# Expert-choice MoE: an expert's list two experts ahead, its rows gathered one ahead and turned inside the preceding down product

## Chip, cores and metric

The kernel runs on one core of one Trainium2 chip. The metric is the device time of one execution in microseconds (us), the median of the runs.

## The reference, cut to what matters

One encoder layer: a norm, one projection, a mixture of dilated attention and a gated recurrence, an output projection, and then a mixture of experts in which each expert picks its own tokens. The change lies in this last part alone. S is 2048 tokens, D is 1024, there are 16 experts of hidden width 1024, and each takes cap = 256 tokens.

```python
def expert_choice_moe(h, w_router, w_gate, w_up, w_down):
    cap = max(1, CAPACITY_FACTOR * S // N_EXPERTS)
    logits = jnp.einsum('bsd,de->bse', h, w_router)
    aff = jax.nn.softmax(logits, axis=-1)
    gate, idx = lax.top_k(aff.transpose(0, 2, 1), cap)
    xin = jax.vmap(lambda hb, ib: hb[ib])(h, idx)
    hid = silu(einsum('becd,edf->becf', xin, w_gate)) * einsum('becd,edf->becf', xin, w_up)
    y = jnp.einsum('becf,efd->becd', hid, w_down) * gate[..., None]
    return jnp.zeros_like(h).at[bidx, idx].add(y)
```

## The kernel before, in words

Some 1680 us go by before the experts: norm and projection, recurrence, attention, output projection, router, and a search that finds for every expert the value that its 256th token has. Nothing in that part is touched. It leaves `post`, which holds for every token and expert the place in the expert's list (or none), `vals`, which holds token numbers and router weights in bf16 pieces, and `h2_d`, the normed tokens in DRAM.

Each expert then goes through these steps, which the names below refer to.

- **List** (`lists`, lines 1014 to 1035). For each of 16 groups of tokens VectorE compares `post` with a ramp and so makes a one-hot matrix `oh` (L1022), and TensorE multiplies two halves of it with `vals` (L1024, 32 small products into a bank of `mpt`). VectorE copies the sums out (`lv`, L1029) and forms the token numbers `ix` (L1032) and the weights `gate` (L1033, L1034).
- **Gather** (`gather`, L1041). Two indirect DMAs, issued from GpSimd (POOL), fetch 128 rows of 4 KB each from `h2_d` into the tiles `xg`.
- **Turning** (`xt_of`, lines 1046 to 1057). TensorE transposes the 2 x 8 blocks of `xg` into `mpt`, four to a bank (L1053); ScalarE writes the high part `xh` (L1055), VectorE the rest `xl` (L1056). Products are made of high and low parts, three for each pair of operands.
- **Gate product** (L1096 to L1098). Eight blocks `fb` of 128 hidden columns, each 2 x 24 products of 256 columns into one bank of `mpg` (two banks). After each block ScalarE takes the silu and VectorE the product `sg` (L1100, L1101), and the two write its parts `hh` and `hl` (L1102, L1103).
- **Down product** (L1129 to L1131). Eight blocks of 12 products of 512 columns, into the four banks of `mpy`. Then `add_rows` scales the result by `gate` (L1108, L1109) and adds it to the output by an indirect DMA from POOL (L1110).
- **Weights** (`w_split`). SP loads 1 MB at a time into `mraw` (three buffers), ScalarE writes the high part `mhi` (L1083), VectorE the low part `mlo` (L1084); six buffers each, two for every block of the gate product, one for every block of the down product.

The order on each engine is made by a scheduler: it simulates the program with its own cost model and lets the ready instruction that stands earliest in the code go first, as far as buffers are free. On the chip each engine then runs its own fixed order, and waits where an operand is late. In the code, list, gather and turning of expert e + 1 all stand ahead of expert e's products:

```python
nxt = ready(0)
for e in range(16):
    cur = nxt
    if e + 1 < 16:
        nxt = ready(e + 1)
    expert(e, *cur)
```

`ready` is list, gather and turning in a row, so all three are spread over the gate product of expert e, and the turning sits there at the place that the simulated gather allowed. The one-hots have three buffers, `xg` has three, `ix` and `gate` three.

Of the kernel before, what the change touches and what calls it, by code (L numbers as in the profile page):

```python
# [45 lines left out]
def encoder_layer(ctx, tc, x, norm1_w, w_in, q_norm_w, k_norm_w, lb_f, lb_b, o_norm_w, w_out,  # L46
# [4 lines left out]
    class Lane:  # L51
        """A range of scheduling priorities (lower goes first) for one stream of instructions."""
# [48 lines left out]
    # ones with a zero at the start of each chunk of 128  # L101
# [6 lines left out]
    def rsqrt(y, a, tmp):  # L108
        """y = a ** -0.5 to fp32 accuracy; a, y, tmp of one shape."""
        act.activation(y, a, AF.Ln)  # L110
        act.activation(y, y, AF.Exp, scale=-0.5)
        dve.tensor_mul(tmp, y, y)
        dve.scalar_tensor_tensor(tmp, tmp, -0.5, a, op0=OP.mult, op1=OP.mult)
        dve.scalar_tensor_tensor(y, tmp, 1.5, y, op0=OP.add, op1=OP.mult)

# [9 lines left out]
    def phase0(g):  # L125
        """tokens 256 g to 256 g + 255, scaled and turned; the low parts as lo_d has them"""
# [31 lines left out]
    # W columns  # L158
    AQ, AK, AV, HQ, HF, HB, HI, HG = [512 * i for i in range(8)]

    def prep(cols, kc):
        """hi and lo parts of two 128-column blocks of W_in with the norm's weight, k block kc"""
# [9 lines left out]
    def evac_qk(u):  # L172
        """columns of two heads' queries and keys: each head's normalised"""
# [30 lines left out]
    def project(cols, kind, ev, begin=False):  # L204
        """one unit of 256 columns; kind "t": tokens on partitions, "f": columns on partitions"""
# [59 lines left out]
    LEVELS = (64, 32, 16, 8, 4, 2, 1)  # L265

    def hg_setup(p):
# [20 lines left out]
        # lower bounds: row 0 of a softmax over two rows, per (direction, head)  # L288
# [25 lines left out]
    def hg_head(p, T, h):  # L314
# [7 lines left out]
        def gates(g, d):  # L322
            """ln f and softplus(z) of direction d; the latter gives the log of the key, ln(1 - lb) - softplus(z)"""
# [25 lines left out]
        # backward direction: E is the sum over the chunk's earlier positions; states after each chunk  # L349
# [22 lines left out]
        for g in range(4):  # L372
# [34 lines left out]
            def level(m):  # L407
                """key and query factors of both directions for pairs in opposite halves of 2m positions; m = 0:
                pairs of a position with itself"""
# [91 lines left out]
    def att_setup(p):  # L501
# [22 lines left out]
        # a column of ones after the values gives the denominators  # L524
# [5 lines left out]
    def att_load(p, T, h, g):  # L530
        """queries and keys of head h: tokens 512 g to 512 g + 511"""
        u, s2 = h // 2, h % 2
        for j in range(2):
            # each row twice, for both halves of the partitions
# [7 lines left out]
    def att_values(T, h, g):  # L542
        # keys of pattern 0 and 1 in blocks of 128, shifted by 64
# [13 lines left out]
    def att_turn(T, g):  # L557
        """columns on partitions: the query's high and low parts, the key's each twice"""
# [18 lines left out]
    def att_head(p, T, h):  # L577
# [8 lines left out]
        def unit(pat, n):  # L586
            """queries' first and stride, keys' first, first and last column, key blocks"""
# [56 lines left out]
        def four(pat, n4, nst):  # L644
            """four units of 128 queries: numerators, denominators and negated maxima"""
# [6 lines left out]
        # partition p of pattern 2 has tokens 16 p + r, of pattern 1 512 g + 4 p + r, of pattern 0 128 n + p;  # L652
        # they are put together in the order of pattern 1
        for g in range(4):
# [5 lines left out]
            # the next head's columns take their places as this head leaves them  # L660
# [41 lines left out]
    def op_setup(op):  # L702
# [8 lines left out]
        # the lower and the upper 16 bits of the gates, as numbers  # L711
# [12 lines left out]
    def op_mm(T, c, half, src, bank):  # L724
        """adds the contribution of mixed's column half to src's tokens"""
# [32 lines left out]
    def op_tile(T, c):  # L758
# [21 lines left out]
        # the norm's scale of a token comes after the product  # L780
# [110 lines left out]
    # the digits' candidates; the third enters negated and half a step lower  # L891
# [39 lines left out]
    def search(v, digits):  # L931
        """the largest whole number that at least CAP of an expert's numbers reach, in base 4"""
        cand, cur = kk[:, digits - 1, :], None
        for i in range(digits - 1, -1, -1):
# [5 lines left out]
            # twice the count less 256, a whole number of at most 256  # L940
# [26 lines left out]
    # the upper bits; then the lower ones among those whose upper bits are the ones found, above or below them the rest  # L967
# [7 lines left out]
    # places: the strictly greater, then those equal as long as there are places  # L975
# [38 lines left out]
    def lists(e):  # L1014
        """token indices and gates of expert e's slots"""
        pl = pt2()
        n = 0
        for hf in range(2):
            for sg in range(8):
                col = e * 8 + sg  # L1020
                oh = mp.tile([128, CAP], BF, name="oh", bufs=3)
                dve.tensor_scalar(oh, iotb, post[:, hf * 128 + col:hf * 128 + col + 1], None, op0=OP.is_equal)  # L1022
                for sh in range(2):
                    pe.matmul(pl[:, sh * 8:sh * 8 + 5], oh[:, sh * 128:(sh + 1) * 128], vals[:, hf, col, :],  # L1024
                              start=n == 0 and sh == 0, stop=n == 15, skip_group_check=True)
                n += 1
# [3 lines left out]
        ix = mp.tile([128, 2], I32, name="ix", bufs=3)  # L1030
        gt_ = mp.tile([128, 2], F32, name="gate", bufs=3)
# [3 lines left out]
        return ix, gt_  # L1035

    def gather(ix):
        xg = []
        for s in range(2):
            t = mp.tile([128, D], F32, name="xg", bufs=3)  # L1040
            pool.indirect_dma_start(out=t, out_offset=None, in_=h2_d,  # L1041
                                    in_offset=bass.IndirectOffsetOnAxis(ap=ix[:, s:s + 1], axis=0))
            xg.append(t)
        return xg

    def xt_of(xg):
        xh = mp.tile([128, KC, 256], F32R, name="xh", bufs=2)
        xl = mp.tile([128, KC, 256], F32R, name="xl", bufs=2)
        for kq in range(4):
            p = pt2()  # L1050
            for j in range(4):
                k, s = kq * 2 + j // 2, j % 2
                pe.transpose(p[:, j * 128:(j + 1) * 128], xg[s][:, k * 128:(k + 1) * 128], ident)  # L1053
            pv_ = p.rearrange("p (k t) -> p k t", k=2)
            act.activation(xh[:, kq * 2:kq * 2 + 2, :], pv_, AF.Copy)  # L1055
            dve.tensor_sub(xl[:, kq * 2:kq * 2 + 2, :], pv_, xh[:, kq * 2:kq * 2 + 2, :].bitcast(F32))  # L1056
        return xh, xl
# [3 lines left out]
    def w_raw(e, kind, i):  # L1061
        """raw weights: gate / up, two 128-column blocks; down, two 128-row blocks"""
# [24 lines left out]
    def expert(e, xh, xl, ix, gate):  # L1087
        hh = mp.tile([128, KC, 256], F32R, name="hh", bufs=1)
        hl = mp.tile([128, KC, 256], F32R, name="hl", bufs=1)
        for fb in range(KC):  # L1090
# [12 lines left out]
            dve.tensor_sub(hl[:, fb, :], sg, hh[:, fb, :].bitcast(F32))  # L1103
        py = [mps.tile([128, 512], F32, name="mpy", bufs=4) for _ in range(4)]
# [8 lines left out]
        # the last expert's second half comes later, so that the first half's rows are added meanwhile  # L1113
        lag = 3 if e == 15 else 0
        wd = {}
        for fb in range(KC + lag):
# [3 lines left out]
            for s in range(2):  # L1120
# [5 lines left out]
                for n in range(2):  # L1126
# [4 lines left out]
                    pe.matmul(o, hl[:, f, ts], hi[:, cs], start=False, stop=f == KC - 1)  # L1131
            if fb == KC - 1:
                add_rows(0)
        add_rows(1)

    def ready(e):
# [36 lines left out]
```

## Time and profile before

| | us |
|---|---|
| runs | 2863.09, 2871.4, 2881.84 |
| median | 2871.4 |
| profiled execution, first to last instruction | 2869.1 |
| TensorE busy in it | 2746.1 (96%) |
| experts: first gate product to last down product | 1680.6 to 2855 |

No time of its own is given for the profiled execution beside its span; the span lies between the lowest and the highest of the three runs, 2.3 us below their median. A busy TensorE in the profile need not be one at its peak: a product that starts while the one before it still runs counts once, and what shows the rate is the distance from one start to the next.

### The profile page before, as it was taken

Reading aid. Unit: us, or ns where it says so; the run is one execution under the profiler, and the core shown is the slowest. Engines: PE = TensorE matmul, PEld = TensorE weight load, DVE = VectorE, ACT = ScalarE, POOL = GpSimd, SP = SyncE. Lnnn points to the kernel's source line nnn. Section 1 sums busy time; section 2 is a strip of 40 time slices with the busy share of each in tenths; the row PEclk is TensorE's granted clock in tenths of the full one; section 3 lists DMA queues with packets and bytes.
Section 4 is the critical chain, followed back from the end, with each engine's and each line's share of the span. In section 5 each row is a group of like instructions: output and inputs, shape, how many; then the busy total and the mean of one; then the engine's idle time right before and its main releaser. Section 6 shows DMA issues by size and latency. Waiting matters only on the chain. (4 is left out here: it accounts for less than half of the span.)

```text
span 2869.1 us, 59634 instructions
## 1 busy us (share of the span) xinstructions
PE 2746.1 (96%) x23462; PEld 2585.8 (90%) x23462; DVE 1780.8 (62%) x4396; ACT 1456.3 (51%) x2829; POOL 131.2 (5%) x157
## 2 busy tenths in 40 slices
PE   8999999999999999999999769999999999999998
PEld 8999998999999999988998669999989999999997
DVE  6637887888865446755666665555555555555553
ACT  6636666676655444634455434444444444444442
POOL 0000000000000000000000000000000000000000
PEclk9999999999999999989999879999999999999999
DMA  9877767777686554645548436666666666666663
GB/s 301 259 243 215 235 209 222 215 222 231 206 236 186 148 141 132 173 136 164 155 110 291 139 113 193 198 203 205 206 205 186 197 198 199 205 204 201 200 202 105
DMA packets 557064, 558.75 MB, mean 195 GB/s; under 512 B 142944, under 2 KB 507488, under 8 KB 556784
## 3 DMA queue, kind: packets, MB, share of 16 engines
q1 hardware_dynamic: 547248, 521.31, 58.2%
q0 software_dynamic: 9536, 33.64, 5.4%
q8 instruction: 184, 3.01, 0.4%
q14 instruction: 96, 0.79, 0.1%
HBM read 453.92 MB, written 100.93 MB: 193 GB/s over the span
## 5 line engine op out<-in xcount | busy, mean ns | idle before, releaser
L1084 DVE TENSOR_TENSOR mlo<-mraw,mhi 128x1024 fp32r<-128x1024 f32 x384 | 470.2, 1225 | 399.9 <-ACT mhi L1083 399.5
L1083 ACT ACTIVATE mhi<-mraw 128x1024 fp32r<-128x1024 f32 x384 | 406.8, 1060 | 517.7 <-PE mpg L1097 328.0
L1096 PE MATMUL mpg<-xh,mhi 128*128 128x256 f32 x2048 | 584.6, 286 | 0.0
L1097 PE MATMUL mpg<-xl,mhi 128*128 128x256 f32 x2048 | 582.6, 285 | 0.0
L1098 PE MATMUL mpg<-xh,mlo 128*128 128x256 f32 x2048 | 579.8, 283 | 0.0
L1096 PEld LDWEIGHTS mpg<-xh,mhi 128*128 128x128 f32 x2048 | 387.5, 189 | 0.5 <-ACT xh L1055 0.4
L1097 PEld LDWEIGHTS mpg<-xl,mhi 128*128 128x128 f32 x2048 | 386.8, 189 | 0.0
L1098 PEld LDWEIGHTS mpg<-xh,mlo 128*128 128x128 f32 x2048 | 386.5, 189 | 0.0
L236 PE MATMUL pm<-whi,hth 128*128 128x256 f32 x1280 | 367.9, 288 | 12.8 <-ACT est L200 9.7
L237 PE MATMUL pm<-wlo,hth 128*128 128x256 f32 x1280 | 366.3, 286 | 3.6 <-DVE wlo L169 3.3
L238 PE MATMUL pm<-whi,hlo 128*128 128x256 f32 x1280 | 366.7, 287 | 0.0
L236 PEld LDWEIGHTS pm<-whi,hth 128*128 128x128 f32 x1280 | 245.3, 192 | 15.8 <-ACT est L200 12.0
L237 PEld LDWEIGHTS pm<-wlo,hth 128*128 128x128 f32 x1280 | 245.2, 192 | 5.8 <-DVE wlo L169 5.0
L238 PEld LDWEIGHTS pm<-whi,hlo 128*128 128x128 f32 x1280 | 245.0, 191 | 0.4
L238 PE MATMUL pm<-hth,wlo 128*128 128x256 f32 x768 | 220.6, 288 | 4.2 <-DVE wlo L169 4.2
L236 PE MATMUL pm<-hth,whi 128*128 128x256 f32 x768 | 220.8, 288 | 2.4 <-ACT est L200 2.3
L237 PE MATMUL pm<-hlo,whi 128*128 128x256 f32 x768 | 219.3, 286 | 0.0
L1131 PE MATMUL mpy<-mhi,hl 128*128 128x512 f32 x512 | 202.9, 396 | 0.0
L1130 PE MATMUL mpy<-mlo,hh 128*128 128x512 f32 x512 | 202.9, 396 | 0.0
L1129 PE MATMUL mpy<-mhi,hh 128*128 128x512 f32 x512 | 202.3, 396 | 0.0
L641 PEld LDWEIGHTS pn<-vp,eT 128*128 128x128 f32 (+1 forms) x1280 | 168.0, 194 | 15.9 <-DVE eT L622 2.6
L641 PE MATMUL pn<-vp,eT 128*128 128x65 f32 (+1 forms) x1280 | 179.8, 278 | 2.5 <-DVE eT L622 2.1
(328 smaller groups left out, 5436.8 us busy)
## 6 DMA issues: line engine op xcount, KB each, us to landing
hlo<-lo_d SPq DMA_DIRECT2D x480, 256.0 KB, 4.1
mraw<-in_w_expert_gate_dram SPq DMA_DIRECT2D x64, 1024.0 KB, 5.2
mraw<-in_w_expert_up_dram SPq DMA_DIRECT2D x64, 1024.0 KB, 5.3
mraw<-in_w_expert_down_dram SPq DMA_DIRECT2D x64, 1024.0 KB, 5.2
wraw<-in_w_in_dram SPq DMA_DIRECT2D x128, 128.0 KB, 4.2
out_dram<-oxt SPq DMA_DIRECT2D x32, 512.0 KB, 4.0
pf_d<-est SPq DMA_DIRECT2D x96, 128.0 KB, 3.8
cb<-num_d SPq DMA_DIRECT2D x32, 264.0 KB, 3.1
```

The costliest lines, as they stand in the source:

```text
L236: pe.matmul(o, l[0], r[0], start=kc == 0, stop=False)
L237: pe.matmul(o, l[0], r[1], start=False, stop=False)
L238: pe.matmul(o, l[1], r[0], start=False, stop=kc == KC - 1)
L641: pe.matmul(pnum[:, n0 % 4 + j, :], eT[:nk, c:c + 128], vp[:nk, b, :], start=i == 0, stop=i == nb - 1)
L1083: act.activation(hi, src, AF.Copy)
L1084: dve.tensor_sub(lo, src, hi.bitcast(F32))
L1096: pe.matmul(o, hi[:, k, :], xh[:, k, :], start=k == 0, stop=False)
L1097: pe.matmul(o, hi[:, k, :], xl[:, k, :], start=False, stop=False)
L1098: pe.matmul(o, lo[:, k, :], xh[:, k, :], start=False, stop=k == KC - 1)
L1129: pe.matmul(o, hh[:, f, ts], hi[:, cs], start=f == 0, stop=False)
L1130: pe.matmul(o, hh[:, f, ts], lo[:, cs], start=False, stop=False)
L1131: pe.matmul(o, hl[:, f, ts], hi[:, cs], start=False, stop=f == KC - 1)
```

## The change

The list of expert e + 2 is now made during expert e, in two halves of eight one-hots and 16 small products each, placed after blocks 2 and 5 of the gate product (`lists_part`). The gather of expert e + 1 stands at the start of expert e, with its indices long made. The turning of expert e + 1 stands in four pieces after blocks 1 to 4 of expert e's down product (`xt_part`). Before the first expert stand list 0, gather 0, list 1 and the turning of expert 0. There are eight buffers for one-hots, and four each for `xg`, `ix` and `gate`. The diff also takes comments out, which moves line numbers by nothing up to L1011.

```diff
-    def lists(e):
-        pl = pt2()
-        n = 0
-        for hf in range(2):
-            for sg in range(8):
-                col = e * 8 + sg
-                oh = mp.tile([128, CAP], BF, name="oh", bufs=3)
...
+    lst = {}
+
+    def lists_part(e, part):
+        if part == 0:
+            lst[e] = pt2()
+        pl = lst[e]
+        ohs = []
+        for sg in range(8):
+            col = e * 8 + sg
+            oh = mp.tile([128, CAP], BF, name="oh", bufs=8)
+            dve.tensor_scalar(oh, iotb, post[:, part * 128 + col:part * 128 + col + 1], None, op0=OP.is_equal)
+            ohs.append((oh, col))
+        for sg, (oh, col) in enumerate(ohs):
+            for sh in range(2):
+                pe.matmul(pl[:, sh * 8:sh * 8 + 5], oh[:, sh * 128:(sh + 1) * 128], vals[:, part, col, :],
+                          start=part == 0 and sg == 0 and sh == 0, stop=part == 1 and sg == 7, skip_group_check=True)
+        if part == 0:
+            return
...
-        ix = mp.tile([128, 2], I32, name="ix", bufs=3)
-        gt_ = mp.tile([128, 2], F32, name="gate", bufs=3)
+        ix = mp.tile([128, 2], I32, name="ix", bufs=4)
+        gt_ = mp.tile([128, 2], F32, name="gate", bufs=4)
...
-            t = mp.tile([128, D], F32, name="xg", bufs=3)
+            t = mp.tile([128, D], F32, name="xg", bufs=4)
...
-    def xt_of(xg):
-        xh = mp.tile([128, KC, 256], F32R, name="xh", bufs=2)
-        xl = mp.tile([128, KC, 256], F32R, name="xl", bufs=2)
-        for kq in range(4):
-            p = pt2()
...
+    def xt_part(xt, xg, kq):
+        xh, xl = xt
+        p = pt2()
...
-    def expert(e, xh, xl, ix, gate):
+    def expert(e, xt, nxt):
+        xh, xl = xt
+        ix, gate = lst[e]
+        xt1 = xt_tiles() if nxt else None
...
+            if fb in (2, 5) and e + 2 < 16:
+                lists_part(e + 2, fb // 3)
...
+            if nxt and 1 <= fb < 5:
+                xt_part(xt1, nxt, fb - 1)
...
+    lists_part(0, 0)
+    lists_part(0, 1)
+    rows = gather(lst[0][0])
+    lists_part(1, 0)
+    lists_part(1, 1)
+    xt = xt_tiles()
+    for kq in range(4):
+        xt_part(xt, rows, kq)
     for e in range(16):
-        cur = nxt
-        if e + 1 < 16:
-            nxt = ready(e + 1)
-        expert(e, *cur)
+        rows = gather(lst[e + 1][0]) if e < 15 else None
+        xt = expert(e, xt, rows)
```

What the scheduler makes of it is shown at three places. First TensorE where the next expert's rows are turned (`mpt<-ident,xg`). Before, in the middle of the gate product (`mpg`) of an expert:

```order
L1098 MATMUL mpg<-xh,mlo 128x256
L1096 MATMUL mpg<-xh,mhi 128x256
L1053 MATMUL mpt<-ident,xg 128x128 x6
L1097 MATMUL mpg<-xl,mhi 128x256
L1098 MATMUL mpg<-xh,mlo 128x256
```

Now, in the down product (`mpy`):

```order
L1143 MATMUL mpy<-mlo,hh 128x512
L1144 MATMUL mpy<-mhi,hl 128x512
L1061 MATMUL mpt<-ident,xg 128x128 x4
L1142 MATMUL mpy<-mhi,hh 128x512
L1143 MATMUL mpy<-mlo,hh 128x512
```

The 16 transposes of an expert moved from pieces of 2, 6, 4 and 4 in the gate product to four pieces of 4 in the down product. The 32 list products (`mpt<-vals,oh`) moved with the same count from six pieces in the gate product of each of the first 15 experts to two pieces of 16 in the gate products of experts 1 to 13, four pieces in expert 0, and none in expert 14.

Second, VectorE ahead of the first expert, from the finished places (`post`) to the first rows' low part (`xl`). Before:

```order
L996 COPY post<-pb 128x256
L1022 TENSOR_SCALAR oh<-iotb,post 128x256 x18
L1029 COPY lv<-mpt 128x2x5
L1022 TENSOR_SCALAR oh<-iotb,post 128x256
L1032 SCALAR_TENSOR_TENSOR ix<-lv 128x2
L1033 TENSOR_TENSOR gate<-lv 128x2
L1034 TENSOR_TENSOR gate<-gate,lv 128x2
L1056 TENSOR_TENSOR xl<-mpt,xh 128x512 x4
```

Now:

```order
L996 COPY post<-pb 128x256
L1025 TENSOR_SCALAR oh<-iotb,post 128x256 x23
L1035 COPY lv<-mpt 128x2x5
L1025 TENSOR_SCALAR oh<-iotb,post 128x256 x7
L1038 SCALAR_TENSOR_TENSOR ix<-lv 128x2
L1039 TENSOR_TENSOR gate<-lv 128x2
L1025 TENSOR_SCALAR oh<-iotb,post 128x256 x7
L1040 TENSOR_TENSOR gate<-gate,lv 128x2
```

The first expert's indices `ix` stood behind 19 one-hots and now stand behind 30, since those of list 1 go in between.

Third, VectorE in the gate product of an expert, around the silu products (`sg`). Before:

```order
L1022 TENSOR_SCALAR oh<-iotb,post 128x256 x3
L1084 TENSOR_TENSOR mlo<-mraw,mhi 128x1024
L1022 TENSOR_SCALAR oh<-iotb,post 128x256 x3
L1084 TENSOR_TENSOR mlo<-mraw,mhi 128x1024
L1101 TENSOR_TENSOR sg<-sg,mpg 128x256
L1022 TENSOR_SCALAR oh<-iotb,post 128x256 x3
L1103 TENSOR_TENSOR hl<-sg,hh 128x256
```

Now, where the `sg` shown is that of block 2:

```order
L1114 TENSOR_TENSOR hl<-sg,hh 128x256
L1025 TENSOR_SCALAR oh<-iotb,post 128x256 x8
L1091 TENSOR_TENSOR mlo<-mraw,mhi 128x1024
L1112 TENSOR_TENSOR sg<-sg,mpg 128x256
L1091 TENSOR_TENSOR mlo<-mraw,mhi 128x1024
L1114 TENSOR_TENSOR hl<-sg,hh 128x256
```

The one-hots stand in rows of eight, those of a list's second half right behind the `hl` of block 1, ahead of a weight split and of the `sg` of block 2; their buffers come free with the list products that TensorE has after block 2. On POOL the pair of gathers for expert e + 2 stands between the output additions of experts e - 1 and e, so behind nothing later than expert e - 1; before, the pair for expert e + 1 stood at that place.

## Rows read from the trace of the kernel before

**Rows 1.** Page, part 1: busy us (share of the span) and instructions of each engine

```profile
PE 2746.1 (96%) x23462; PEld 2585.8 (90%) x23462; DVE 1780.8 (62%) x4396; ACT 1456.3 (51%) x2829; POOL 131.2 (5%) x157
```

**Rows 2.** Windows: expert 8's and expert 15's gate stage, expert 8's down stage

```profile
core 0: us, PE busy (x) PEld busy (x) DVE busy (x) ACT busy (x) POOL busy (x), PEclk, DMA share, GB/s
2273.32:2324.04 50.72, 49.40 (x433) 48.95 (x433) 31.54 (x56) 23.50 (x35) 5.60 (x4) 1.00 0.69 212
2786.52:2832.60 46.08, 46.08 (x386) 46.08 (x385) 25.32 (x32) 21.20 (x31) 3.20 (x2) 1.00 0.65 195
2324.04:2346.52 22.48, 22.48 (x98) 17.89 (x96) 10.75 (x11) 10.13 (x12) 0.00 (x0) 1.00 0.54 180
```

**Rows 3.** Waits of PE from 1700 us on: total, times, longest

```profile
PE mpt L1053 <- DMA xg<-h_d,ix: 23.1, 15, 2.5
```

**Rows 4.** Timeline of PE at the gather of expert 9's rows

```profile
2296.86 0.28 PE L1096 MATMUL mpg<-xh,mhi 128*128 128x256 f32 x1
2298.46 0.87 PE L1053 MATMUL mpt<-ident,xg 128*128 128x128 f32 x6 [1.32 <-DMA xg<-h_d,ix]
2299.09 0.36 PE L1097 MATMUL mpg<-xl,mhi 128*128 128x256 f32 x1
2299.29 0.28 PE L1098 MATMUL mpg<-xh,mlo 128*128 128x256 f32 x1
```

**Rows 5.** Timeline of PE at a piece of list products

```profile
2277.17 0.31 PE L1024 MATMUL mpt<-vals,oh 128*128 128x5 bf16 x6
2277.33 0.37 PE L1096 MATMUL mpg<-xh,mhi 128*128 128x256 f32 x1
2277.53 0.28 PE L1097 MATMUL mpg<-xl,mhi 128*128 128x256 f32 x1
```

**Rows 6.** Windows: after two long gather waits, and an undisturbed stretch

```profile
2003.40:2006.80 3.40, 3.40 (x18) 3.40 (x17) 2.63 (x4) 1.83 (x4) 0.00 (x0) 0.50 0.05 22
2150.10:2153.50 3.40, 2.76 (x13) 2.77 (x14) 1.20 (x2) 1.19 (x2) 0.00 (x0) 0.51 0.47 182
2310.00:2313.40 3.40, 3.40 (x31) 3.40 (x30) 1.56 (x2) 1.89 (x3) 0.00 (x0) 1.00 0.99 349
1631.30:1682.50 51.20, 16.10 (x100) 10.47 (x101) 35.23 (x173) 13.91 (x40) 7.93 (x6) 0.50 0.09 32
```

**Rows 7.** Timeline of DVE ahead of the first expert

```profile
1667.20 3.80 DVE L1022 TENSOR_SCALAR oh<-iotb,post 128x256 bf16<-128x256 bf16 x18
1671.19 0.15 DVE L1032 SCALAR_TENSOR_TENSOR ix<-lv 128x2 int32<-128x2 f32 x1
```

**Rows 8.** Timeline of PE ahead of the first expert

```profile
1676.96 0.69 PE L1053 MATMUL mpt<-ident,xg 128*128 128x128 f32 x2 [6.09 <-DMA xg<-h_d,ix]
1679.06 1.54 PE L1053 MATMUL mpt<-ident,xg 128*128 128x128 f32 x6 [1.41 <-DMA xg<-h_d,ix]
```

**Rows 9.** Timeline of POOL: gathers of experts 0 and 1

```profile
1672.26 1.11 POOL L1041 DMA_INDIRECT xg<-h_d,ix  x1 [32.25 <-DVE gate L1034]
1673.67 0.96 POOL L1041 DMA_INDIRECT xg<-h_d,ix  x1 [0.30 <-issue]
1701.55 0.94 POOL L1041 DMA_INDIRECT xg<-h_d,ix  x1 [26.92 <-DVE gate L1034]
1702.79 1.64 POOL L1041 DMA_INDIRECT xg<-h_d,ix  x1 [0.30 <-issue]
```

**Rows 10.** Tile xg from 1660 us on: issue to landing of its gathers

```profile
DMA to landing us min/median/max: 4.3/5.6/9.6
```

**Rows 11.** Lines from 1700 us on: busy us, mean ns, idle before

```profile
L1084 DVE TENSOR_TENSOR mlo<-mraw,mhi 128x1024 fp32r<-128x1024 f32 x374 | 458.0, 1225 | 396.6 <-ACT mhi L1083 396.4
L1101 DVE TENSOR_TENSOR sg<-sg,mpg 128x256 f32<-128x256 f32 x126 | 52.3, 415 | 0.0
L1131 PEld LDWEIGHTS mpy<-mhi,hl 128*128 128x128 f32 x512 | 96.4, 188 | 23.5
```

**Rows 12.** Waits of DVE from 1700 us on

```profile
DVE oh L1022 <- PE mpt L1024: 48.0, 56, 1.3
```

More of the change, by code (lines that the diff above doesn't have):

```diff
@@ L1012, in pt2 @@
         return mps.tile([128, 512], F32, name="mpt", bufs=2)
-    def lists(e):
-        pl = pt2()
-        n = 0
-        for hf in range(2):
-            for sg in range(8):
-                col = e * 8 + sg
-                oh = mp.tile([128, CAP], BF, name="oh", bufs=3)
[L1022 to L1026, printed above, removed]
+    lst = {}
[15 more added lines that the diff above has]
+            return
         lv = mp.tile([128, 2, 8], F32, name="lv", bufs=2)
@@ L1034, in lists @@
         dve.tensor_add(gt_, gt_, lv[:, :, 4])
-        return ix, gt_
+        lst[e] = ix, gt_
     def gather(ix):
@@ L1044, in gather, with xt_tiles @@
         return xg
-    def xt_of(xg):
-        xh = mp.tile([128, KC, 256], F32R, name="xh", bufs=2)
-        xl = mp.tile([128, KC, 256], F32R, name="xl", bufs=2)
-        for kq in range(4):
-            p = pt2()
[L1051 to L1057, printed above, removed]
+    def xt_tiles():
+        return [mp.tile([128, KC, 256], F32R, name=n, bufs=2) for n in ("xh", "xl")]
+    def xt_part(xt, xg, kq):
+        xh, xl = xt
+        p = pt2()
+        for j in range(4):
+            k, s = kq * 2 + j // 2, j % 2
+            pe.transpose(p[:, j * 128:(j + 1) * 128], xg[s][:, k * 128:(k + 1) * 128], ident)
+        pv_ = p.rearrange("p (k t) -> p k t", k=2)
+        act.activation(xh[:, kq * 2:kq * 2 + 2, :], pv_, AF.Copy)
+        dve.tensor_sub(xl[:, kq * 2:kq * 2 + 2, :], pv_, xh[:, kq * 2:kq * 2 + 2, :].bitcast(F32))
     raws = {}
@@ L1134, in expert @@
         add_rows(1)
-    def ready(e):
-        ix, gate = lists(e)
-        return (*xt_of(gather(ix)), ix, gate)
-    nxt = ready(0)
+        return xt1
+    lists_part(0, 0)
[6 more added lines that the diff above has]
+        xt_part(xt, rows, kq)
     for e in range(16):
-        cur = nxt
-        if e + 1 < 16:
-            nxt = ready(e + 1)
-        expert(e, *cur)
+        rows = gather(lst[e + 1][0]) if e < 15 else None
+        xt = expert(e, xt, rows)
 _INS = ["x", "norm1_w", "w_in", "attn_q_norm_w", "attn_k_norm_w", "hgrn_lb_fwd", "hgrn_lb_bwd",
```

## Prediction

> **What bounds the kernel now.** I read the page's busy shares first, then the stages as windows, the waits of TensorE in the expert part, and last the timeline at each wait. TensorE is busy for 96% of the span [rows 1], so what can be gained is a gap in its stream of instructions or a product that takes longer to follow the one before; another engine's time counts only where TensorE waits for it. Expert 15 makes no list and turns no rows for a successor: its 384 gate products take 46.08 us, 0.12 us from start to start, without idle time. Expert 8 runs the same products with a list of 32 and 16 transposes among them and takes 50.72 us; VectorE is busy for 31.54 us of it, ScalarE for 23.50 [rows 2]. So 4.64 us go to list, turning and what they bring with them.
>
> The timeline splits these. The 6 list products of a piece take 0.16 us, 0.027 each, so 0.9 for 32; the gate product behind the piece needs 0.20 us to its successor instead of 0.12, so each piece costs 0.08 more than its work [rows 5]. In the turning, a gate product starts at 2296.86, and the next instruction, a transpose, at 2298.46: 1.60 us where 0.12 is usual, so 1.48 lost, of which the profile counts 1.32 as idle (the 0.16 between is the product's own tail). The six transposes behind it take 0.63 us, about 0.1 each, and the product after them again 0.20 [rows 4]. Together: 0.9 list, 1.5 transposes, 1.48 wait, and 10 pieces (6 of the list, 4 of the turning) at 0.08, which makes 4.7 beside the 4.64 measured. Nothing large is missing.
>
> The wait is the gather's. From 1700 us on it is TensorE's only wait: 15 times, 23.1 us in all, longest 2.5 [rows 3]. All three steps of `ready` fall into one gate product, the list ends in the middle of it, and the transposes come before the rows land. After the two longest waits, of 2.1 us and more, the granted clock fell to 0.50, that is 1.2 GHz, for 3.4 us each [rows 6]: 18 products started where 31 do at full clock.
>
> **What the change removes.**
> 1. The 15 waits. Now the list of expert e + 2 is complete after block 5 of e's gate product, its gather follows, and its rows are first touched in the down product of e + 1. Between lie two blocks of gate product, a down product of 22.48 us and another gate product of 46 us; a gather lands in 9.6 us at most [rows 2, 10]. On POOL nothing that comes later than that stands ahead of it. So the waits go whole: 23.1 plus 15 x 0.16 = 25.5 us. What is late next is nothing on TensorE that the trace shows.
> 2. The two falls of the clock that followed them: 3.4 us at half rate lose 1.7 each, 3.4 us.
> 3. Pieces of lists. Before there are 15 x 6 = 90; now 4 in expert 0, and 2 in each of 13 experts, 30. The 60 fewer give 60 x 0.08 = 4.8 us.
> 4. List 1 runs before the first expert, while TensorE waits for gather 0 (6.09 us of idle time [rows 8]): its 32 products, 0.9 us, leave the gate product.
>
> **What it adds and moves.**
> 5. Before the first expert VectorE comes to `ix` behind 30 one-hots instead of 19. 18 of them took 3.80 us, 0.211 each [rows 7]; 11 x 0.211 = 2.3 us later starts the gather, and all that waits for it: TensorE's idle time grows by that. From below: TensorE now runs twice as many small products just before, in a stretch that is at half clock until 1682.5 [rows 6]; were the clock back earlier, up to half of the 3.4 us between the first full piece of transposes at 1679.06 and 1682.5, so 1.7, would be given back. From above: gather 1 is now issued right behind gather 0 and could draw its landing out from the median to the longest seen, by 4.0 us [rows 10]. Bounds 0.6 and 6.3; I take 2.3, the part that the order fixes.
>    The Trainium skill, SBUF — State Buffer, section SBUF: two separate sides, says that GpSimd cannot write descriptors for its DMAs while VectorE runs an instruction that holds the port the two share; the one-hots that now run while gather 0 is issued would then delay it. The rows are mixed. Three of the four first gathers kept POOL for 0.94 to 1.11 us and one, beside weight splits, for 1.64 [rows 9]: at worst 0.7 for each of two gathers, so the change would save 1.4 us less by the rule, and by the three rows nothing less. Of a later expert's gathers the rule changes nothing, since they have tens of us to spare.
> 6. The turning moves with its four pieces from the gate to the down product; a transpose costs the same there. The trace shows no transpose among down products, so the price of a piece is bounded: 0, if the long down product (0.234 us from start to start, 22.48/96) hides the switch, or a whole weight load of 0.188 us, if none of it is hidden [rows 11]. Against 0.08 now, 60 pieces bring between -4.8 and +6.5 us. I take the price in the gate product, the nearest thing seen, so 0.
> 7. ScalarE and VectorE now write `xh` and `xl` in the down stage: 23.50 - 21.20 = 2.3 us of ScalarE, and 31.54 - 25.32 less 16 one-hots at 0.211, so 2.8, of VectorE, by the gate stages with and without. They are busy in the down stage for 10.13 and 10.75 of 22.48 us [rows 2], so this is hidden; the last piece stands 33 down products (7.7 us) ahead of the next expert's first gate product. Without that cover, each us that `xl` is late would cost 15.
> 8. Eight one-hots in a row instead of three. Those of a list's second half wait for the buffers that TensorE's list products after block 2 give back, and behind them on VectorE stand a weight split and the `sg` of block 2, which frees the bank that block 4 needs. By the rows: list piece 0.45 us, eight one-hots 1.7, split 1.2, `sg` 0.4, so `sg` is done 3.8 us after block 2. Block 4 starts after the list piece and 48 x 0.119 = 5.7, so at 6.2. Margin 2.4 us; I take 0.
>
> **The sum.** -25.5 - 3.4 - 4.8 - 0.9 + 2.3 = -32.3 us. Against the profiled span, 2869.1, that is 2836.8; what lies around the span isn't given, and the median of the runs is 2.3 above it, so 2839.1. With the bounds of 5 and 6 the saving lies between 38.8 (-4.8 and -1.7) and 21.8 (+6.5 and +4.0); where the median run has no falls of the clock to lose, it is 3.4 less, 18.4.
>
> **Rivals.**
> A. *The waits move rather than go.* TensorE gets new, shorter stalls: `xl` of the last piece late for the next expert, or `sg` late by a little under a us, twice an expert (28 places). For it: VectorE is the busiest engine after TensorE, and a weight split waited for ScalarE for 396 us in all [rows 11]. Against: margins of 2.4 and some 4 us. Half a us at 28 places is 14 us: 2853, within 1%.
> B. *Slower: VectorE's queue behind the one-hots.* One-hots already wait for TensorE's list products (56 times, 48.0 us), though never over 1.3 us each [rows 12]; a row of eight would wait for the end of a whole block. If the split between them and `sg` then has to wait for weights that TensorE frees only a block later, `sg` comes after block 4 should start. It decides from 2.4 us on; the saving is used up at 1.2 us beyond that (28 x 1.15 = 32), and a split held up for a whole block more (5.7 us late, 3.3 beyond the margin) would cost 92 us: 2839 + 92 = 2931. Against it: the split that stands there is for block 5, whose buffer is free once block 2 is done.
>    The Trainium skill speaks for this rival too: PSUM — Partial Sum Buffer, section Engine vs sequencer instructions, has VectorE's queue as strictly first in, first out, so that nothing passes a one-hot that waits. Rows 12 agree with it as far as they go, with waits of at most 1.3 us.
> C. *The change doesn't do what it says*: the gather is still late, since POOL holds it behind an output addition. Then only terms 3 to 5 are left, -3.4 us: 2868, no change. Against: POOL's order has only the additions of expert e - 1 ahead of the gather for e + 2.
>
> **How the numbers follow.** About 1% (28.7 us, below 2842.7 or above 2900.1) is what a measurement of this kernel can tell from no change. The forecast, a saving of 18 to 39 us, has 0.80; A 0.11; B 0.04; C 0.05. The forecast's own bounds straddle the 1%: its centre lies 3.6 us beyond, and since the runs before lie 9 us to either side of their median, I give three quarters of it to faster. So faster 0.60; same 0.80 - 0.60 + 0.11 + 0.05 = 0.36; slower 0.04. For the range, the bounds of the sum give 2871.4 - 38.8 = 2832.6 to 2871.4 - 18.4 = 2853; with the spread of the runs, some 6 us for a median of three, 2827 to 2859. That leaves out the slow rival and C.
>
> **What would show it.** Right: no wait of TensorE for `xg` after the first expert's; a gate stage of about 47.1 us (46.08 + 0.9 + 2 x 0.08) and a down stage of 24.3 (22.48 + 1.5 + 4 x 0.08) in experts 1 to 13; clock at full from the first expert on; first transposes about 2.3 us later than now. Wrong: a wait of TensorE for `sg` at blocks 4 and 7 or for `xl` at the start of an expert (A, B), a down stage over 24.7 (term 6), gathers that still land after their transposes are due (C), falls of the clock without a gather wait ahead of them (term 2).

## The result, and the profile after

| | before | after |
|---|---|---|
| device time, median | 2870.0 us (2863.1 to 2881.8) | 2829.1 us (2827.8 to 2840.3) |
| ratio, with 95% interval | | 0.9864 [0.9834, 0.9895] |
| the profiled execution, and its span | span 2869.1 us | 2828.0 us, span 2825.4 us |
| VectorE's first one-hot to the end of the span | 1201.9 us | 1169.5 us |

The changed kernel is faster by 1.4%, and the whole interval lies beyond the 1% that the prediction took as the least that can be told from no change. By the medians it saves 40.9 us, where 32.3 had been forecast: more than the forecast's upper bound of 38.8, though the time itself, 2829.1 us, lies inside the range of 2827 to 2859. The last row of the table is the one to compare with the forecast: the change begins with VectorE's first one-hot (at 1667.20 in [rows 7]), and all that comes ahead of it is the same code on every engine. I call that instant the mark.

TensorE is still busy throughout; its busy time fell by 17.2 us against [rows 1], less than the span's 43.7, and its share rose to 97%.

```profile
PE 2728.9 (97%) x23462; PEld 2574.3 (91%) x23462; DVE 1775.3 (63%) x4396; ACT 1453.8 (51%) x2829; POOL 128.3 (5%) x157
```

The same windows as in [rows 2]: expert 8's gate stage, expert 15's, and expert 8's down stage, of the changed kernel. The columns are start and end, length, busy time and count of each engine, then the granted clock.

```profile
core 0: us, PE busy (x) PEld busy (x) DVE busy (x) ACT busy (x) POOL busy (x), PEclk, DMA share, GB/s
2245.00:2292.05 47.05, 47.05 (x417) 46.95 (x416) 28.81 (x52) 21.19 (x31) 5.19 (x4) 1.00 0.73 226
2742.89:2788.96 46.07, 46.07 (x386) 46.07 (x384) 25.29 (x32) 21.18 (x31) 3.12 (x2) 1.00 0.65 195
2292.05:2316.26 24.21, 24.21 (x115) 19.64 (x113) 13.16 (x15) 12.30 (x16) 0.00 (x0) 1.00 0.52 172
```

The gate stage has 1.0 us more than expert 15's, not 4.6, and no idle time; the down stage has 1.73 us more than before, and none either. The turning is now in the third row: 15 instructions of VectorE instead of 11, 16 of ScalarE instead of 12.

TensorE's waits from 1640 us on that name the gather. From 1700 us on, where [rows 3] had 15 of them, the view has no row at all; these two stand ahead of the first expert.

```profile
PE mpt L1061 <- DMA xg<-h_d,ix: 6.6, 2, 5.1
```

TensorE's timeline at a list piece (after block 2 of expert 8) and at a turning piece (in its down stage); columns: start, duration, instruction, count.

```profile
2262.15 0.28 PE L1109 MATMUL mpg<-xh,mlo 128*128 128x256 f32 x1
2262.27 0.56 PE L1029 MATMUL mpt<-vals,oh 128*128 128x5 bf16 x16
2262.69 0.37 PE L1107 MATMUL mpg<-xh,mhi 128*128 128x256 f32 x1
2262.89 0.28 PE L1108 MATMUL mpg<-xl,mhi 128*128 128x256 f32 x1
...
2297.67 0.60 PE L1061 MATMUL mpt<-ident,xg 128*128 128x128 f32 x4
2298.03 0.48 PE L1142 MATMUL mpy<-mhi,hh 128*128 128x512 f32 x1
2298.34 0.39 PE L1143 MATMUL mpy<-mlo,hh 128*128 128x512 f32 x1
```

A list piece now has 16 products, not 6 as in [rows 5], and takes 0.42 us to the next gate product, which itself needs 0.20 to its successor. Four transposes take 0.36 us, and the down product behind them 0.31 to its successor, 0.08 over its usual 0.234. There is no hole like the 1.60 us in [rows 4].

The start of the experts, to be held against [rows 7 to 9]: VectorE, TensorE and POOL.

```profile
1655.93 4.59 DVE L1025 TENSOR_SCALAR oh<-iotb,post 128x256 bf16<-128x256 bf16 x23
1660.44 0.16 DVE L1035 COPY lv<-mpt 128x10 f32<-128x10 f32 x1
1660.51 1.45 DVE L1025 TENSOR_SCALAR oh<-iotb,post 128x256 bf16<-128x256 bf16 x7
1661.88 0.15 DVE L1038 SCALAR_TENSOR_TENSOR ix<-lv 128x2 int32<-128x2 f32 x1
1662.03 1.46 DVE L1025 TENSOR_SCALAR oh<-iotb,post 128x256 bf16<-128x256 bf16 x7
```

```profile
1656.27 6.51 PE L1029 MATMUL mpt<-vals,oh 128*128 128x5 bf16 x64 [0.90 <-DVE oh L1025]
1667.87 0.66 PE L1061 MATMUL mpt<-ident,xg 128*128 128x128 f32 x2 [5.10 <-DMA xg<-h_d,ix]
1670.04 1.54 PE L1061 MATMUL mpt<-ident,xg 128*128 128x128 f32 x6 [1.51 <-DMA xg<-h_d,ix]
```

```profile
1662.96 1.18 POOL L1047 DMA_INDIRECT xg<-h_d,ix  x1 [34.21 <-DVE oh L1025]
1664.44 0.96 POOL L1047 DMA_INDIRECT xg<-h_d,ix  x1 [0.30 <-issue]
1665.70 0.94 POOL L1047 DMA_INDIRECT xg<-h_d,ix  x1 [0.30 <-issue]
1666.94 0.94 POOL L1047 DMA_INDIRECT xg<-h_d,ix  x1 [0.31 <-issue]
```

`ix` comes 5.95 us after the mark, where it came after 3.99, and the first transposes 11.94 us after it instead of 9.76. So 2.2 us are lost here. Both gathers are issued in a row, at 0.94 to 1.18 us each; only the first of the four issues lies beside one-hots, since VectorE's last one ends at 1664.22.

### The profile page after: what moved, and what is told of

It reads as the page before. It is cut to its first block, busy times and chain, and to the rows that moved or that the text cites. A ratio compares the mean times of both kernels' runs of the same rounds, so it can differ in the third digit from the quotient of the medians.

```text
span 2825.4 us, 59470 instructions
## 1 busy us (share of the span) xinstructions
PE 2728.9 (97%) x23462; PEld 2574.3 (91%) x23462; DVE 1775.3 (63%) x4396; ACT 1453.8 (51%) x2829; POOL 128.3 (5%) x157
## 4 chain that ended last, share of the span: by engine, by line
PE 83%; DMA 8%; DVE 7%; ACT 2%; issue 1%; SPq 0%; POOLq 0%; POOL 0%; DVEq 0%; ACTq 0%
PE mpg L1107 9%; PE mpg L1109 9%; PE mpg L1108 9%; PE pm L236 6%; PE pm L238 6%; PE pm L237 6%; PE pn L641 5%; PE mpy L1142 4%; PE mpy L1144 4%; PE mpy L1143 4%; PE pa L607 2%; PE pa L608 2%; PE pb L618 2%; PE pm L749 2%; PE pm L750 2%; PE pm L751 2%
## 5 line engine op out<-in xcount | busy, mean ns | idle before, releaser
L1108 PE MATMUL mpg<-xl,mhi 128*128 128x256 f32 x2048 | 576.6, 282 | 0.0
```

The lines of the kernel that those rows point to most:

```text
L1108: pe.matmul(o, hi[:, k, :], xl[:, k, :], start=False, stop=False)
```

## The experiments

All profiles are of one execution each. "Mark to end" is read as in the table above; the expectations count from the copy into `post` just ahead of the first one-hot, which adds 0.5 us. The stages are those of expert 8.

| kernel | gate stage | down stage | mark to end | mark at | median us (runs) | ratio to before |
|---|---|---|---|---|---|---|
| before | 50.7 | 22.5 | 1201.9 | 1667.2 | 2870.0 (4) | |
| before, again | | | 1197.7 | 1664.7 | 2876.5 (8) | 1.0003 [0.9972, 1.0034] |
| after | 47.05 | 24.21 | 1169.5 | 1655.9 | 2829.1 (4) | 0.9864 [0.9834, 0.9895] |
| after, again | 47.06 | 24.21 | 1168.2 | 1666.4 | 2838.8 (6) | 0.9880 [0.9856, 0.9904] |
| list alone | 48.75 | 22.48 | 1169.0 | 1667.1 | 2840.7 (4) | 0.9884 [0.9823, 0.9945] |
| turning alone | 47.27 | 24.38 | 1172.9 | 1672.0 | 2843.9 (4) | 0.9882 [0.9827, 0.9937] |
| turning in two pieces | 47.08 | 24.23 | 1169.9 | 1662.4 | 2836.4 (4) | 0.9869 [0.9814, 0.9924] |
| one-hots twice | | | 1170.2 | 1661.5 | 2834.8 (1) | |
| one-hots four times | | | 1170.7 | 1667.6 | 2840.3 (1) | |
| `ix` first | 47.04 | 23.74 | 1159.3 | 1681.6 | 2834.7 (6) | 0.9850 [0.9818, 0.9882] |
| `ix` first, again | | 23.73 | 1158.3 | 1664.4 | 2833.9 (4) | 0.9871 [0.9849, 0.9892] |
| weights 96 bytes up | 47.04 | 23.74 | 1161.2 | 1663.3 | 2826.5 (1) | |
| rows 96 bytes down | 47.08 | 23.72 | 1161.7 | 1665.1 | 2829.1 (1) | |
| weights 32 bytes up | 46.24 | 24.16 | 1154.6 | 1673.3 | 2830.9 (1) | |

**Which part takes the waits away.** My theory: either part alone does, since each puts tens of us between a gather and its transposes. The rival: the list must come two experts ahead. Beside two kernels with one part each, the kernel before ran once more, unedited, as the measure of the spread.

> The kernel before, profiled a second time. In the first pair of profiles the places (L996, VectorE's copy of the finished places) were ready at 1666.7 us before and at 1655.4 after, though the change touches nothing ahead of them; from there to the end it took 1202.4 and 1170.0 us. Theory (the 11.3 us ahead of the places are chance): this time the places come at some other time, anywhere from about 1650 to 1672 us, and the rest takes 1199 to 1206 us with 15 gather waits of 21 to 26 us in all. Rival (the change speeds that part too, by where its tiles lie): the places come at 1665 to 1669 us again.

The list alone: made two experts ahead in two pieces, but the rows turned in the gate product as before.

```diff
             if fb in (2, 5) and e + 2 < 16:
                 lists_part(e + 2, fb // 3)
+            if nxt and 1 <= fb < 5:
+                xt_part(xt1, nxt, fb - 1)
...
-            if nxt and 1 <= fb < 5:
-                xt_part(xt1, nxt, fb - 1)
```

> The change with the turning left in the gate product (after blocks 1 to 4 of the preceding expert), the list two ahead in halves and the gather one ahead as changed. Theory (the gather's lead is what counts, and either part of the change gives it): no gather wait after the first expert's, 96 down products in 22.48 us, a gate stage 1.7 us longer than in the change, and from the places to the end 1170 us, within 1 of the change. Rival (the down product is the better place for the turning): 1175 us or more, by gaps around the transposes in the gate product.

The turning alone: the list is made one expert ahead by the function of before, the turning stands in the down product.

```diff
-            if fb in (2, 5) and e + 2 < 16:
-                lists_part(e + 2, fb // 3)
...
     for e in range(16):
+        if e < 15:
+            lst[e + 1] = lists(e + 1)
```

> The list as before (one ahead, in six pieces, three one-hot buffers, gather right after it), only the turning moved into the down product. Theory (either part alone gives the gather its lead): no gather wait after the first expert's; against the change 60 more pieces of list products at 0.077 (+4.6 us), list 1 back in the gate product (+0.9), and the first gather 2.3 us earlier: 1173.2 us from the places to the end. Rival (the list must be two experts ahead): the gather is late for the down product too, waits of 20 us or more in all, 1190 us or more.

Measured: neither kernel has a wait of TensorE after 1700 us. Turning alone takes 29.0 us off mark to end; the list alone does all that the change does (1169.0 against 1169.5). The windows of both, gate and down stage, show where the turning sits: 1.7 us of it in the first kernel's gate stage, in the second's down stage.

```profile
2255.81:2304.56 48.75, 48.75 (x434) 48.66 (x432) 31.21 (x56) 23.60 (x35) 5.19 (x4) 1.00 0.72 217
2304.56:2327.04 22.48, 22.48 (x99) 18.08 (x97) 10.77 (x11) 10.14 (x12) 0.00 (x0) 1.00 0.56 186
```

```profile
2261.30:2308.57 47.27, 47.27 (x417) 47.02 (x414) 28.60 (x52) 21.12 (x31) 5.59 (x4) 1.00 0.73 224
2308.57:2332.95 24.38, 24.38 (x121) 19.62 (x119) 13.34 (x15) 12.47 (x16) 0.00 (x0) 1.00 0.54 173
```

(The second's down stage also holds one list piece of six products, which before is counted with the gate stage.) So the place of the turning decides nothing once its rows are there in time, and the list two experts ahead is worth 1172.9 - 1169.5 = 3.4 us: the pieces saved, less the later first gather. By the second execution of the changed kernel (1168.2) it would be 4.7, so that figure is good to about 1.3 us.

The kernel before, again, had 15 gather waits of 21.5 us in all, the longest 1.8, and no fall of the clock after them; its mark to end is 4.2 us shorter. Counted as its expectation counts, that is 1198.2 us, below the 1199 to 1206 that were expected. Its places came at 1664.2 us, inside the range for chance but only 0.8 us outside the rival's, so this run alone settles little of what lies ahead of the mark.

**What a turning piece costs.** The theory, by the prediction's 0.08 us a piece: two pieces of eight transposes instead of four of four save that twice an expert.

```diff
-            if nxt and 1 <= fb < 5:
-                xt_part(xt1, nxt, fb - 1)
+            if nxt and fb in (1, 4):
+                xt_part(xt1, nxt, fb // 4 * 2)
+                xt_part(xt1, nxt, fb // 4 * 2 + 1)
```

> The change with the turning in two pieces of 8 transposes instead of four of 4, after blocks 1 and 4 of the down product. Theory (a piece costs 0.077 us over its work): 30 pieces fewer, 2.3 us less, 1167.7 us from the places to the end, a down stage of 24.05 instead of 24.2 us. Rival (a piece costs nothing, what is lost goes by transposes): 1170 us.

It saved nothing: 24.23 us against 24.21. TensorE's timeline of this kernel shows why.

```profile
2304.25 1.03 PE L1061 MATMUL mpt<-ident,xg 128*128 128x128 f32 x8
2305.04 0.48 PE L1142 MATMUL mpy<-mhi,hh 128*128 128x512 f32 x1
2305.36 0.39 PE L1143 MATMUL mpy<-mlo,hh 128*128 128x512 f32 x1
```

Eight transposes take 0.79 us, four took 0.36. From one to the next it is 0.109 us; only the last of a piece is followed after 0.028, and then the down product needs 0.08 more. 0.028 + 0.08 is about 0.109 again, so every transpose costs that, first or last of a piece, and 16 cost 1.74: the 1.73 that the down stage gained. Only the list products have a price by the piece.

**How near VectorE is (rival B).** The one-hots of lists 3 to 15 were written two and four times, which adds work of VectorE and nothing else.

```diff
-            dve.tensor_scalar(oh, iotb, post[:, part * 128 + col:part * 128 + col + 1], None, op0=OP.is_equal)
+            for _ in range(2 if e > 2 else 1):
+                dve.tensor_scalar(oh, iotb, post[:, part * 128 + col:part * 128 + col + 1], None, op0=OP.is_equal)
```

> Each one-hot of lists 3 to 15 is written twice, which puts 13 of them, not 8, ahead of block 2's sg on VectorE and adds 16 x 0.206 = 3.3 us of its time to an expert. Theory (margin): sg of block 2 comes 1.0 us later, of the 2.8 that are left before block 4's first product; TensorE waits for nothing more than before and the experts take 1170 us within 1. Rival (VectorE's queue is the bound after the change): TensorE waits for sg or for an evicted bank in each of 13 experts, by 1 us or more, and the experts take 1183 us or more.

> Each one-hot of lists 3 to 15 is written four times: 48 x 0.206 = 9.9 us more of VectorE in an expert, beside 27 us of it in a gate stage of 47. Theory (margin): VectorE has the room, but the list's products come a block or more later, and where sg is set behind 16 to 20 one-hots its margin is used up; TensorE waits under 1 us in an expert, and the experts take 1170 to 1183 us. Rival: VectorE's queue is the bound at once: more than 5 us in an expert, 1235 us or more.

TensorE waits for nothing after the first expert in either. The window of one whole expert, in the changed kernel and in that with four:

```profile
2245.00:2316.26 71.26, 71.26 (x530) 66.59 (x528) 41.97 (x67) 33.49 (x47) 5.19 (x4) 1.00 0.66 208
```

```profile
1971.81:2043.16 71.35, 71.35 (x530) 66.72 (x529) 50.70 (x115) 33.48 (x47) 6.93 (x4) 1.00 0.66 207
```

In this expert, 8.7 us more of VectorE cost 0.1 us. The dose is softer than meant: the scheduler sets `sg` behind 13 one-hots in both kernels and moves the rest behind it. So VectorE's load is no bound at this dose, while a single long row of one-hots ahead of `sg` was not tried.

**`ix` first, and what came with it.** Term 5 says that the first gather waits for VectorE's queue. List 1's places get a zero made of list 0's `ix` added, so that its one-hots can't go ahead.

```diff
+    nil = rt.tile([128, 1], F32, name="nil", bufs=1)
+    dve.tensor_scalar(nil, lst[0][0][:, 0:1], 0.0, None, op0=OP.mult)
+    post2 = rt.tile([128, 2, 8], F32, name="post2", bufs=1)
+    dve.tensor_scalar(post2, post.rearrange("p (h c) -> p h c", h=2)[:, :, 8:16], nil, None, op0=OP.add)
...
-            dve.tensor_scalar(oh, iotb, post[:, part * 128 + col:part * 128 + col + 1], None, op0=OP.is_equal)
+            place = post2[:, part, sg:sg + 1] if e == 1 else post[:, part * 128 + col:part * 128 + col + 1]
+            dve.tensor_scalar(oh, iotb, place, None, op0=OP.is_equal)
```

> List 1's places are added to a zero that is made from list 0's ix, so that none of list 1's one-hots can stand ahead of ix on VectorE: ix then follows 16 one-hots, not 30. Nothing else is moved. Theory of the fifth term (what ix waits for is VectorE's queue): 14 one-hots of 0.206 us = 2.9 us come off the way to the first gather, so from the end of the untouched part to the first product of expert 0 it takes 13.3 us, not 16.2, and from there to the end 1167 us, not 1170; list 1 then is made while the gather is on its way, and its products fit into the wait before expert 0, which is over 5 us. Rival: the one-hots that now run beside the descriptors' writing, or list 1's products standing ahead of the transposes, cost as much as was won, and it takes 16 us again.

> The changed kernel once more, nothing edited. Theory: of the 43.7 us by which the profiled span fell, 32.4 belong to the experts and about 11 to chance in the part ahead of them, which is the same code in both kernels and ended anywhere from 1655.4 to 1671.5 us in the six profiles so far. So the part ahead ends in that range again and most likely above 1655.4, the experts and what follows it take 1170 us again within 1, and the median lies at 2832 to 2842. Rival: the change also makes the part ahead faster (through the layout of its memory, say): then that part ends at 1655 again, and the median is 2829 within 3.

VectorE's timeline of the kernel with `ix` first:

```profile
1681.59 3.23 DVE L1026 TENSOR_SCALAR oh<-iotb,post 128x256 bf16<-128x256 bf16 x16
1685.12 0.17 DVE L1036 COPY lv<-mpt 128x10 f32<-128x10 f32 x1 [0.31 <-PE mpt L1030]
1685.33 0.16 DVE L1039 SCALAR_TENSOR_TENSOR ix<-lv 128x2 int32<-128x2 f32 x1
...
1685.98 4.21 DVE L1026 TENSOR_SCALAR oh<-iotb,post 128x256 bf16<-128x256 bf16 x21
```

`ix` comes 3.74 us after the mark instead of 5.95, the first gate product 13.2 instead of 15.4 to 15.7: term 5 is won back, a little less than the 2.9 us that were expected. The rival's first half, that one-hots beside the gather's issue cost as much, didn't come true. The 21 one-hots behind `ix` ran from 1685.98 to 1690.19, and both issues of gather 0 lie beside them:

```profile
1686.41 1.11 POOL L1048 DMA_INDIRECT xg<-h_d,ix  x1 [31.99 <-DVE oh L1026]
1687.82 1.05 POOL L1048 DMA_INDIRECT xg<-h_d,ix  x1 [0.30 <-issue]
```

But 10 us were saved, and the down stage, which the edit doesn't touch, fell from 24.21 to 23.74. By the program's addresses the two new tiles had moved the weights' tiles (`mraw`, `mhi`, `mlo`) from 0 to 96 bytes beyond a multiple of 128; `xh`, `xl`, `hh` and `hl` lie 96 beyond one, in the kernels before and after alike. The changed kernel, run again in the same series, kept 24.21; from the places to the end it took 1168.7 us, 0.3 less than its expectation allowed.

**The place in SBUF by itself.** Three kernels get a pad and nothing else: 96 bytes ahead of the weights' tiles, which moves them up; 96 bytes behind the rows' tiles, which moves those down; and 32 bytes (8 numbers instead of 24) ahead of the weights.

```diff
+    pad = rt.tile([128, 24], F32, name="pad", bufs=1)
+    dve.memset(pad, 0.0)
```

```diff
+        if e == 0:
+            pad = mp.tile([128, 24], F32, name="pad", bufs=1)
+            dve.memset(pad, 0.0)
```

> The changed kernel with a pad of 96 bytes in SBUF, which moves the weights' tiles mraw, mhi and mlo 96 bytes up, from 0 to 96 beyond a multiple of 128; the rows' tiles (xh, xl, hh, hl) stay 96 beyond one. In the kernel that made ix first, two small new tiles had moved them in just this way, and its down products followed each other in 229.5 ns, not 234.1. Theory (the place of the weights in SBUF): the down stage takes 23.73 us again, not 24.21, and the experts 1162 to 1164 us with the first gather as late as before (16 us). Rival (something else in that kernel, or its execution): 24.21 us and 1170.

> The changed kernel with a pad of 96 bytes behind the rows' tiles, which moves xh, xl, hh and hl 96 bytes down, to a multiple of 128, where the weights are too. Theory A (what counts is that both operands of a product lie alike): the down stage takes 23.7 us, the experts 1163. Theory B (the weights' own place counts): 24.2 us and 1170. Theory C (a multiple of 128 is bad for whatever lies on it): over 24.2 us.

> The pad is 32 bytes, not 96: the weights' tiles lie 32 beyond a multiple of 128, the rows' tiles 96, so that the operands differ by 64. If what counts is the place within 64 bytes, the down stage takes 23.7 us and the experts 1162; if it is the place within 128 or more, 24.2 us and 1170; if it is graded by the difference, something between.

Down stages of the first two, in this order; then gate and down stage of the third:

```profile
2295.35:2319.09 23.74, 23.74 (x115) 19.59 (x113) 13.08 (x15) 12.28 (x16) 0.00 (x0) 1.00 0.53 173
```

```profile
2297.36:2321.08 23.72, 23.72 (x114) 19.59 (x113) 13.07 (x15) 12.28 (x16) 0.00 (x0) 1.00 0.51 172
```

```profile
2254.57:2300.81 46.24, 46.24 (x417) 46.15 (x416) 28.84 (x52) 21.20 (x31) 5.16 (x4) 1.00 0.75 230
2300.81:2324.97 24.16, 24.16 (x115) 19.60 (x114) 13.16 (x15) 12.30 (x16) 0.00 (x0) 1.00 0.54 172
```

Theory A holds for the down product: with weights and rows equally far beyond a multiple of 128, whichever of them moved, it takes 0.47 us less, in 16 experts 7.5 in all; mark to end fell by 8.3, which is 0.3 more than the first one's expectation allowed, and by 7.8. Each pad ran once, but the stage repeats: the 15 down stages with a turning take 23.69 to 23.74 us in these two kernels, 24.19 to 24.22 in the changed one. With 64 bytes between them none of my three cases came true: the down stage stays at 24.16, and the gate stage falls by 0.8 us, to 14.9 us less from mark to end than in the changed kernel. This distance was made in one way only, so it isn't shown that the distance, and not the weights' own place at 32, is what counts there.

> The kernel that makes ix first and has its weights 96 bytes higher, once more, on another chip. Theory: the experts and what follows take 1160 us within 1 (10 less than in the changed kernel: 2.5 by the earlier gather, 7.7 by the down products), the part ahead ends anywhere from 1655 to 1681, and the median is 2819 to 2835, with a ratio to before of 0.981 to 0.986. Rival (what the place won is lost elsewhere): 1165 or more.

Again 10 to 11 us less from mark to end than the changed kernel: 1158.9 us as the expectation counts, 0.1 under its range. The ratio of 0.9871 lies above the 0.981 to 0.986 that were expected. The medians (2834.7 and 2833.9 against 2829.1 and 2838.8) don't show the gain: they carry the spread of the part ahead of the mark, and the ratios' intervals overlap. By mark to end `ix` first beats both kernels, and the kernel with the weights 32 bytes up does by more; by the device time neither is told from the changed kernel.

## Why the prediction was right

The direction, the mechanism and the sum held. From the mark to the end the profiled execution saved 1201.9 - 1169.5 = 32.4 us; the forecast was 32.3. That they agree to 0.1 is luck: the two profiles of each kernel, taken crosswise, give 28.2 to 33.7.

1. *The waits* (-25.5) and 2. *the falls of the clock* (-3.4): the turning alone, which removes just these, saved 29.0, against 28.9. The second is not there in every execution: before, again, had no fall, and measured against it the first profile after saves 28.2.
3. *Fewer pieces* (-4.8), 4. *list 1 ahead* (-0.9), 5. *the later first gather* (+2.3) make 3.4 less; the list's part measured 3.4. Term 5 by itself was 2.2 at the transposes. The rule weighed there (the Trainium skill, SBUF — State Buffer, section SBUF: two separate sides) would, if a one-hot holds that port, have drawn out the gathers beside the one-hots. Three issues stood beside one-hots, one in the changed kernel and two with `ix` first, and took 1.18, 1.11 and 1.05 us; the others of the first two gathers in these kernels took 0.93 to 0.96, and the one of 1.11 in [rows 9] had none beside it. So these traces show nothing like the 0.7 us for each that was weighed; whether a one-hot holds the port isn't shown. Nor did the clock come back earlier, the lower bound of the term: in this execution it is low for 5.9 us after the first full piece of transposes (1670.04), not for 3.4, and 2.4 us more at half rate cost some 1.2 us beside the 2.2. With both the term is inside its bounds of 0.6 and 6.3. In the changed kernel, run again, it is low for 3.3 us (1680.17 to 1683.50), which by the same reckoning is most of the 1.3 us between the two executions. So the sign that the clock would be full from the first expert on came true 4.3 us after the first gate product in the first execution and 1.7 us after it in the second. The window of the first execution, as in [rows 6]:

```profile
1621.30:1675.90 54.60, 21.59 (x143) 14.97 (x144) 39.55 (x197) 14.05 (x39) 8.62 (x8) 0.50 0.14 49
```

6. *The turning's place* (0, between -4.8 and +6.5): 0. The gate stage came to 47.05 us (forecast 47.1) and the down stage to 24.21 (24.3). The reason given, 0.08 us a piece as in the gate product, was no more than a way to count: a transpose costs 0.109 wherever the piece ends, and two pieces fewer brought nothing.
7. *`xh` and `xl` in the down stage*: hidden, no wait.
8. *Eight one-hots in a row*: `sg` was expected 3.8 us after block 2, with a margin of 2.4. VectorE's timeline of expert 8:

```profile
2262.51 1.66 DVE L1025 TENSOR_SCALAR oh<-iotb,post 128x256 bf16<-128x256 bf16 x8 [0.33 <-PE mpt L1029]
2264.09 1.22 DVE L1091 TENSOR_TENSOR mlo<-mraw,mhi 128x1024 fp32r<-128x1024 f32 x1
2265.22 0.41 DVE L1112 TENSOR_TENSOR sg<-sg,mpg 128x256 f32<-128x256 f32 x1
```

`sg` ends at 2265.63, and block 2's last product at 2262.43: 3.2 us, which leaves 2.9 until block 4. The order of the four was as worked out. One-hots still wait for TensorE, but for 9.1 us in all and 0.4 at most, where [rows 12] have 48.0 and 1.3:

```profile
DVE oh L1025 <- PE mpt L1029: 9.1, 25, 0.4
```

Rival A's waits don't exist, B's price isn't reached, and C's gathers never keep TensorE waiting after the first expert.

What the forecast didn't see is the 11.3 us by which the mark itself came earlier in the profiled pair (1667.2 and 1655.9). Nothing ahead of it was changed, and in the 12 profiles with the change or a part of it the mark lay between 1655.9 and 1681.6; the first profile after is the earliest of all. The granted clock goes with it: over the first 1600 us it was 0.99 in the two of the 12 with the earliest marks, 0.97 in the two with the latest, and 0.98 in the others. The changed kernel first, then the latest:

```profile
0.00:1600.00 1600.00, 1552.32 (x14843) 1481.94 (x14844) 1069.05 (x3163) 902.26 (x2035) 37.84 (x89) 0.99 0.68 203
```

```profile
0.00:1600.00 1600.00, 1543.76 (x14689) 1475.21 (x14690) 1055.35 (x3125) 892.62 (x2007) 38.54 (x89) 0.97 0.67 200
```

The changed kernel, run again, had a median of 2838.8 us, 0.3 from the forecast of 2839.1; the 2829.1 of its first four runs is the lucky end. Why the clock falls in some executions more than in others wasn't tried.

## What to carry to other kernels

Where the bound engine waits for a short chain (list, gather, turn), how long the chain has before its result is needed matters more than the place of the work: here either of the two moves, list or turning, removed the whole wait alone, and the second added only what it saves in switches. Measure such a change from the first instruction that it touches, not by the whole span, if a part ahead of it varies by more than the effect. And compare the addresses of an edited kernel's tiles with those of the kernel before it: a small new tile can shift others and gain more than the edit, as 7.5 us against 2.5 did here.

## What had not been expected of the hardware

- A product's pace changes with the place of its operands in SBUF, for the down product with their place to each other. By the stages, less list (1.0 us) or turning (1.74), over 384 and 96 products: with weights and rows 96 bytes apart (beyond multiples of 128) a 512-column product follows the one before after 0.234 us and a 256-column one after 0.120; 0 apart, after 0.229 and 0.120; 64 apart (one kernel), after 0.234 and 0.118. A kernel with `hh` and `hl` at 0 and `xh` and `xl` at 64 from the weights might have both gains, 16 x (0.47 + 0.81) = some 20 us; that is an estimate from these stages and wasn't tried, and what in the memory causes it stays open.
- In the kernel before, the two gather waits of 2.1 us and more were each followed by 3.4 us at a granted clock of 0.50 [rows 6]. In its second execution the 15 waits were of 1.8 us at most, and the clock stayed at 1.00 behind all of them. Its waits, and the window behind the longest:

```profile
PE mpt L1053 <- DMA xg<-h_d,ix: 21.5, 15, 1.8
2365.50:2372.00 6.50, 6.50 (x56) 6.50 (x57) 3.96 (x6) 4.41 (x8) 0.00 (x0) 1.00 0.25 98
```
